# Seven products of halves in place of eight for the output projection of a hybrid encoder block

## The chip, the cores and the metric

The kernel runs on one core of a Trainium2 chip. A core has five engines with a queue each: TensorE (PE; its weight loads are listed apart as PEld), VectorE (DVE), ScalarE (ACT), GpSimd (POOL) and SyncE (SP), whose queue issues nearly all DMAs. They meet through semaphores only. The metric is the device time of one execution in microseconds (us), the median of several.

## The reference, cut to what matters

One encoder layer over 512 positions of 1024 features in float32. Two token mixers run side by side: a pooling branch and a gated delta rule. The place that is changed is where they come together:

```python
merged = jax.nn.sigmoid(g_pool) * y_pool + jax.nn.sigmoid(g_dn) * y_dn   # y_dn = o @ dn_out
x = x + merged @ w_o[l]                       # (512, 1024) @ (1024, 1024)
h2 = rmsnorm(x, norm2_w[l])
u = dwconv_centered(h2 @ ffn_up[l], ffn_conv_w[l], ffn_conv_b[l])
gate, val = jnp.split(u, 2, axis=-1)
x = x + (jax.nn.silu(gate) * val) @ ffn_down[l]
return rmsnorm(x, final_norm_w)
```

## The kernel before, in words

**Arithmetic.** Every large product is done in three matmuls. An operand is split in a high part (`hi`, a cast to fp32r by ACT) and the rest (`lo`, a subtraction by POOL or DVE); `mm3` adds hi·hi, hi·lo and lo·hi in one PSUM bank. A *triple* below is one call of `mm3`: three matmuls of 128 rows by 128 columns with 512 moving columns.

**Stages around the change.** `po_unit` forms the pooling branch's projection. `do_unit(c)` forms column block c of `o @ dn_out` (8 blocks of 8 triples, PSUM tile `ps_do`), with the tiles of `o` kept in the pool `kq` (tags `kT`, `kk`). Its weights come through `weights`: SP loads 512 KB (`wr_do`), ACT casts it (`wh_do`), POOL makes the rest in two halves (`wl_do`). Then DVE multiplies PSUM with a gate (`gdl`, L1538) and adds the pooling branch (`m1l`, L1541), ACT casts the sum (`m_hi`) and DVE forms its rest (`m_lo`, L1548). Then comes the product with `w_o`: `wo_block` loads `w_o` in eight pieces of 512 KB through the ring of raw weights, ACT casts 16 tiles and POOL makes their 16 rests (`wo_lo`, `wo_kk`, L1586). The tiles of the second half of the columns lie in `kT` and `kk`, which are free once `ps_do` is done. PE forms 4 token tiles x 2 halves of columns, each of 8 triples (`ps_wo`, 192 matmuls), and DVE adds each to x (L1624). Once both halves of a token tile are in, `norm_transpose` norms it over all 1024 features: ACT squares and sums, ACT takes the root, DVE scales (`sq`, 1024 wide, L539), PE turns it in 8 transposes (`pt_b`), and ACT and DVE split it in `h_hi`, `h_lo`. The up-projection (`ps_up`) starts on the first two token tiles, in half-width matmuls, while the last tile is being normed.

**What sets the order.** Nothing is ordered by hand. Each step is recorded as a task (`A` for ACT, `V` DVE, `G` POOL, `M` PE, `L` a DMA) with what it reads and writes, a cost and a key. `Planner.run` lays them out by a list schedule with these costs: among the tasks of an engine that are ready, the lowest key goes first (`FEED` before `EVICT` before `CHAIN` before the rest). What it finds is the fixed order of each engine's queue in the program; on the chip an engine never goes past its next instruction. Buffers of a kind form a ring, and `RINGS` says how many there are.

Of the kernel before, what the change touches and what calls it, by code (L numbers as in the profile page):

```python
# [227 lines left out]
def hybrid_block(  # L228
# [107 lines left out]
    tri = const.tile([P, 2, P], F32, name="tri")  # L336

    def causal(ap, d, pattern, fill):
        sgn = 1 if d == 0 else -1
        pool.affine_select(  # L340
            out=ap, in_=ap, compare_op=ALU.is_ge, fill=fill, base=0,
            pattern=pattern + [[sgn, P]], channel_multiplier=-sgn,
        )

    for d in range(2):
        pool.memset(tri[:, d, :], 1.0)
        causal(tri[:, d, :], d, [], 0.0)
    mask = const.tile([P, 2, P], F32, name="mask")
    for d in range(2):
        pool.memset(mask[:, d, :], 0.0)  # L350
        causal(mask[:, d, :], d, [], NEG)
# [1171 lines left out]
    def do_unit(c):
        box, pp, u = job(
            dn_out[0][:, c * P : (c + 1) * P], KD, lambda k: o_hl[k], lambda k, a, b_: [f"kT{k}", f"kk{k}"], f"do{c}"
# [14 lines left out]
        def plus():  # L1540
            dve.tensor_tensor(out=b["m1"], in0=b["gd"], in1=b["m1"], op=ALU.add)  # L1541

        def hi():
            m_hl[c] = [pools["mg"].tile([P, S], F32R, name=f"m_{n}{c}") for n in ("hi", "lo")]
            act.copy(m_hl[c][0], b["m1"])

        def lo():
            dve.tensor_tensor(out=m_hl[c][1], in0=b["m1"], in1=f32(m_hl[c][0]), op=ALU.subtract)  # L1548
# [15 lines left out]
    wo = {0: [None] * KD, 1: [None] * KD}  # L1564

    def wo_block(hf, kk, u):
        b = {}
# [15 lines left out]

        def lo(j):
            k = 2 * kk + j
            pool.tensor_tensor(out=wo[hf][k][1], in0=b["raw"][:, j, :], in1=f32(wo[hf][k][0]), op=ALU.subtract)  # L1586
# [416 lines left out]
```

## Time and profile before

| | |
|---|---|
| median of 3 runs | 882.44 us (881.97 to 883.57) |
| the profiled execution | 884.96 us, with a span of 883.2 us |
| busy share of the span | PE 99%, PEld 83%, DVE 63%, POOL 57%, ACT 52% |
| mean granted clock of PE | 0.999 |
| matmuls into `ps_do`, start | from 439.2 us to 483.2 us |
| matmuls into `ps_wo`, start | from 483.5 us to 530.0 us |
| first matmul of the up-projection | 530.2 us |

A row of the timeline gives the start in us from the span's start, the duration, the engine, the line, the operation, the tiles (out<-in), the shapes and how many instructions were merged; in brackets stands how long the engine had been idle and what ended it. Matmuls overlap, so their own duration (0.39 us) is longer than the distance from one start to the next.

### The profile page before, as it was taken

What the parts mean: (1) busy time and instruction counts of PE and PEld (TensorE: products, weight loads), DVE (VectorE), ACT (ScalarE), POOL (GpSimd) and SP (SyncE); (2) the same over time, 40 slices, a digit from 0 to 9 for tenths busy, and PEclk for the clock granted to TensorE, in tenths of its full rate; (3) what the DMA queues carried; (4) which work ended last, traced back from release to release, by engine and by line L of the source; (5) the groups of instructions that cost most, each with busy time, mean ns of one, the idle gap of its engine ahead of it and who ended that gap; (6) DMA issues with size and microseconds to landing.
All of it is one profiled execution on the core that took longest, in us unless ns stands there. A gap on an engine that the chain in (4) does not pass through costs nothing. (4 is left out here: it accounts for less than half of the span.)

```text
span 883.2 us, 13747 instructions
## 1 busy us (share of the span) xinstructions
PE 872.4 (99%) x5051; PEld 735.2 (83%) x5051; DVE 554.7 (63%) x985; ACT 457.2 (52%) x759; POOL 499.3 (57%) x438
## 2 busy tenths in 40 slices
PE   8999999999999999999999999999999999999997
PEld 7988888888888787889878888888888888888886
DVE  4657687357568797555544145655665554569996
ACT  5588554335858543345755334444443333465664
POOL 3545455324546654244467806877787764567763
PEclk9999999999999999999999999999999999999999
DMA  7265546404245453224687607666666753365554
GB/s 205 79 197 139 140 119 152 127 26 131 73 118 151 126 146 83 75 75 137 223 258 264 191 1 233 219 207 222 215 203 203 242 172 101 105 203 191 169 175 157
DMA packets 165511, 138.08 MB, mean 156 GB/s; under 512 B 23662, under 2 KB 133051, under 8 KB 165444
## 3 DMA queue, kind: packets, MB, share of 16 engines
q1 hardware_dynamic: 160706, 135.62, 49.4%
q10 hardware_dynamic: 4738, 1.58, 0.8%
q8 instruction: 40, 0.66, 0.3%
q14 instruction: 27, 0.22, 0.1%
HBM read 113.03 MB, written 24.15 MB: 155 GB/s over the span
## 5 line engine op out<-in xcount | busy, mean ns | idle before, releaser
L413 POOL TENSOR_TENSOR wl_up<-wr_up,wh_up 128x512 fp32r<-128x512 f32 x88 | 114.2, 1320 | 52.4 <-ACT wh_up L409 52.4
L389 PE MATMUL ps_up<-h_lo,wh_up 128*128 128x512 f32 (+1 forms) x368 | 139.9, 380 | 0.3 <-DVE h_lo L558 0.3
L388 PE MATMUL ps_up<-h_hi,wh_up 128*128 128x512 f32 (+1 forms) x368 | 139.9, 380 | 0.0
L390 PE MATMUL ps_up<-h_hi,wl_up 128*128 128x512 f32 (+1 forms) x368 | 139.8, 380 | 0.0
L1716 DVE SCALAR_TENSOR_TENSOR c<-ps_up,fw,c 128x511 f32<-128x511 f32 x88 | 66.0, 750 | 101.3 <-ACT c L1710 95.4
L1701 POOL TENSOR_TENSOR tp<-tp 128x512 f32<-128x512 f32 x44 | 60.4, 1373 | 39.7 <-DMA tp<-in_ffn_down_dram 34.6
L1905 POOL TENSOR_TENSOR w_dn<-wr_dn,w_dn 128x512 fp32r<-128x512 f32 x44 | 65.9, 1513 | 28.7 <-ACT w_dn L1902 27.2
L389 PEld LDWEIGHTS ps_up<-h_lo,wh_up 128*128 128x128 f32 x368 | 69.2, 188 | 13.8 <-DVE h_lo L558 0.5
L390 PEld LDWEIGHTS ps_up<-h_hi,wl_up 128*128 128x128 f32 x368 | 69.2, 188 | 13.2
L388 PEld LDWEIGHTS ps_up<-h_hi,wh_up 128*128 128x128 f32 x368 | 69.2, 188 | 13.0
L409 ACT CAST wh_up<-wr_up 128x1024 fp32r<-128x1024 f32 x44 | 46.3, 1052 | 63.3 <-issue 29.3
L1902 ACT CAST w_dn<-wr_dn 128x512 fp32r<-128x512 f32 x69 | 42.4, 621 | 29.5 <-PE dn L390 20.6
L389 PE MATMUL dn<-w_dn,as 128*128 128x512 f32 x141 | 54.2, 385 | 0.0
L388 PE MATMUL dn<-w_dn,as 128*128 128x512 f32 x141 | 54.2, 384 | 0.0
L390 PE MATMUL dn<-w_dn,as 128*128 128x512 f32 x141 | 54.2, 384 | 0.0
L1670 DVE TENSOR_TENSOR as<-a,as 128x512 fp32r<-128x512 f32 (+1 forms) x41 | 41.8, 1044 | 0.1
L413 POOL TENSOR_TENSOR wl_k<-wr_k,wh_k 128x512 fp32r<-128x512 f32 x16 | 20.2, 1286 | 33.5 <-ACT wh_k L409 33.5
L1666 ACT CAST as<-a 128x512 fp32r<-128x512 f32 (+1 forms) x41 | 21.5, 535 | 32.2 <-DVE a L1737 28.6
L413 POOL TENSOR_TENSOR wl_do<-wr_do,wh_do 128x512 fp32r<-128x512 f32 x16 | 26.0, 1647 | 15.3 <-ACT wh_do L409 15.3
L413 POOL TENSOR_TENSOR wl_gp<-wr_gp,wh_gp 128x512 fp32r<-128x512 f32 x16 | 21.9, 1389 | 22.1 <-ACT wh_gp L409 22.1
L413 POOL TENSOR_TENSOR wl_v<-wr_v,wh_v 128x512 fp32r<-128x512 f32 x16 | 21.3, 1353 | 22.6 <-ACT wh_v L409 22.6
L1710 ACT ACTIVATE c<-ps_up,fw 128x512 f32<-128x512 f32 x44 | 33.9, 770 | 0.0
(358 smaller groups left out, 2421.0 us busy)
## 6 DMA issues: line engine op xcount, KB each, us to landing
wr_up<-in_ffn_up_dram SPq DMA_DIRECT2D x44, 512.0 KB, 3.8
tp<-in_ffn_down_dram SPq DMA_DIRECT2D x22, 512.0 KB, 5.8
t_scr<-tp SPq DMA_DIRECT2D x44, 256.0 KB, 2.8
wr_dn<-t_scr SPq DMA_DIRECT2D x20, 512.0 KB, 3.8
wr_dn<-in_ffn_down_dram SPq DMA_DIRECT2D x15, 512.0 KB, 3.6
x<-in_x_dram SPq DMA_DIRECT2D x8, 512.0 KB, 5.4
wr_k<-in_w_in_dram SPq DMA_DIRECT2D x8, 512.0 KB, 4.7
wr_z<-in_w_in_dram SPq DMA_DIRECT2D x8, 512.0 KB, 3.7
```

What stands on the lines that cost most here:

```text
L388: pe.matmul(ps, ahi, bhi, start=first, stop=False)
L389: pe.matmul(ps, ahi, blo, start=False, stop=False)
L390: pe.matmul(ps, alo, bhi, start=False, stop=last)
L409: act.copy(b["hi"], b["raw"])
L413: pool.tensor_tensor(out=b["lo"][:, sl], in0=b["raw"][:, sl], in1=f32(b["hi"][:, sl]), op=ALU.subtract)
L1666: act.copy(sets[p][:, i : i + n, 0, :], src())
L1670: dve.tensor_tensor(out=w[:, :, 1, :], in0=src(), in1=f32(w[:, :, 0, :]), op=ALU.subtract)
L1701: G(cp(512), lambda o=o, x=x, y=y: pool.tensor_tensor(out=w(*o), in0=w(*x), in1=w(*y), op=ALU.subtract), r=[n(*x), n(*y)], w=[n(*o)], key=u)
L1710: act.activation(b[j], box["ps"], AF.Identity, scale=fw[:, 1, ci : ci + 1], bias=fw[:, 3, ci : ci + 1])
L1716: dve.scalar_tensor_tensor(out=y[:, lo:hi], in0=box["ps"][:, lo + sh : hi + sh], scalar=fw[:, k, ci : ci + 1], in1=y[:, lo:hi], op0=ALU.mu ...
L1902: act.copy(b["w"][:, 0, :], raw["t"][:, j, :])
L1905: eng.tensor_tensor(out=b["w"][:, 1, :], in0=raw["t"][:, j, :], in1=f32(b["w"][:, 0, :]), op=ALU.subtract)
```

## The change

`merged` (512 x 1024) and `w_o` (1024 x 1024) are cut in four blocks each. Seven products of combinations of blocks take the place of the eight products of blocks. A product is 2 token tiles x 4 triples of 512 columns. The order of the products is 1, 2, 6, 5, 3, 7, 4 (`W_ORDER`).

- The raw `w_o` no longer passes through the ring; it is loaded into the memory of `h` (`wr_hi`, `wr_lo`), which is free after the last projection of `h`, and its eight loads are paced by `po_unit` and the first two `do_unit`s.
- Combinations of its blocks: 16 subtractions of 512 columns (`wsum`, L1588), 8 of them on DVE and 8 on POOL. 28 casts by ACT (16 before) and 28 rests (`wsplit`, L1604), 23 on POOL and 5 on DVE.
- `merged` stays as one f32 tile `m` (`plus`, L1549). Combinations of its blocks are 8 instructions of DVE (`mcombine`, L1620, two row blocks of 256 tokens at a time), and the operands are split in 15 casts of ACT and 15 rests of DVE (`msplit`, L1632, tile `ms`), where before there were 8 and 8.
- PSUM: products 1, 6, 3 and 4 use two banks of `oo` (tile `wo`), 2, 5 and 7 the ring `pp`. Sums go to x by 12 additions of DVE from PSUM (`wplus`, L1753; 8 before), or first into a tile `wu` (one cast of ACT and two additions of DVE for each token half, L1765), and from there to x by 6 additions of POOL.
- The second norm is taken in two halves of its features: `norm2_first` squares the half that is ready first and lets POOL multiply it with the weight (L1697), `norm2_rest` squares the other half, takes the root, scales the first half on ACT and the other on DVE (L1712, 512 wide). The transposes are as many as before.
- In `do_unit` the sigmoid, the multiplication and the addition have other keys, the POOL half of `wl_do` is planned 0.2 us longer (`more`), the weights of the first up-projection block have another key, and the masks `tri`, `mask` lie in another pool.

**POOL, from the weights of dn_out's third column block on.** Before:

```order
L413 TENSOR_TENSOR wl_do_4590<-wr_do_4437,wh_do_4589 128x512 x2
L413 TENSOR_TENSOR wl_do_4617<-wr_do_4499,wh_do_4616 128x512 x2
L413 TENSOR_TENSOR wl_do_4665<-wr_do_4554,wh_do_4664 128x512 x2
L413 TENSOR_TENSOR wl_do_4709<-wr_do_4625,wh_do_4708 128x512 x2
L413 TENSOR_TENSOR wl_do_4753<-wr_do_4655,wh_do_4752 128x512 x2
L1586 TENSOR_TENSOR wo_lo_4793<-wo_r_4743,wo_hi_4792 128x512
L413 TENSOR_TENSOR wl_do_4801<-wr_do_4699,wh_do_4800 128x512 x2
```

and now, from two rests of `w_o` ahead of the same place:

```order
L1604 TENSOR_TENSOR ws_lo_4587<-wr_hi,ws_hi_4586 128x512
L415 TENSOR_TENSOR wl_do_4599<-wr_do_4444,wh_do_4598 128x512 x2
L415 TENSOR_TENSOR wl_do_4631<-wr_do_4498,wh_do_4630 128x512 x2
L1604 TENSOR_TENSOR ws_lo_4612<-wr_hi,ws_hi_4611 128x512
L1604 TENSOR_TENSOR ws_lo_4620<-wr_hi,ws_hi_4619 128x512
L1604 TENSOR_TENSOR ws_lo_4676<-wr_hi,ws_hi_4675 128x512
L415 TENSOR_TENSOR wl_do_4685<-wr_do_4547,wh_do_4684 128x512 x2
L1604 TENSOR_TENSOR ws_lo_4696<-wr_hi,ws_hi_4695 128x512
L415 TENSOR_TENSOR wl_do_4735<-wr_do_4643,wh_do_4734 128x512 x2
L1604 TENSOR_TENSOR ws_lo_4761<-wr_hi,ws_hi_4760 128x512
L415 TENSOR_TENSOR wl_do_4781<-wr_do_4668,wh_do_4780 128x512 x2
```

Work on `w_o` now stands between the weights of dn_out's blocks. From `wl_do` of the second block to `wl_up` of the second up-projection block, ends included, POOL has 60 instructions of 512 columns (35 before): 14 `wl_do`, one `o_lo`, 23 rests and 8 combinations of `w_o`, 6 additions to x, 4 multiplications of the norm, 4 `wl_up`.

**DVE, from the eviction of dn_out's last column block on.** Before:

```order
L1538 TENSOR_TENSOR gdl_4782<-ps_do_4845,gdl_4782 128x512
L1541 TENSOR_TENSOR m1l_4815<-gdl_4782,m1l_4815 128x512
L1548 TENSOR_TENSOR m_lo_4915<-m1l_4815,m_hi_4914 128x512
L1624 TENSOR_TENSOR x_0_4573<-ps_wo_4892,x_0_4573 128x512
L1624 TENSOR_TENSOR x_1_4574<-ps_wo_4934,x_1_4574 128x512
```

and now:

```order
L1546 TENSOR_TENSOR gdl_4828<-ps_do_4867,gdl_4828 128x512
L1753 TENSOR_TENSOR x_1_4571<-wo,x_1_4571 128x512
L1604 TENSOR_TENSOR ws_lo_4969<-wr_lo,ws_hi_4968 128x512
L1549 TENSOR_TENSOR m<-gdl_4828,m1l_4882 128x512
L1632 TENSOR_TENSOR ms_4979<-m,ms_4979 128x2x256
L1620 TENSOR_TENSOR m<-m 128x2x256
L1632 TENSOR_TENSOR ms_4887<-m,ms_4887 128x256
L1620 TENSOR_TENSOR m<-m 128x2x256 x2
L1753 TENSOR_TENSOR x_0_4570<-ps_wo_4971,x_0_4570 128x512
L1632 TENSOR_TENSOR ms_4979<-m,ms_4979 128x2x256
```

Before, three instructions (two of them with both inputs in SBUF) lay between the last `ps_do` and the last operand of the product with `w_o`. Now the second half of product 6's left operand (`ms_4979`) stands behind eleven, eight of them with both inputs in SBUF.

**PE, where product 6 starts** (`wo<-wq_...,ms_4979`) and product 2 ends (`ps_wo_4971`, `ps_wo_4995<-...,ms_4887`). Now, with none like it before:

```order
L391 MATMUL ps_wo_4995<-ws_hi_4760,ms_4887 128x512
L389 MATMUL wo<-wq_kT_4878,ms_4979 128x512
L390 MATMUL wo<-wq_kk_4879,ms_4979 128x512
L391 MATMUL wo<-wq_kT_4878,ms_4979 128x512
L389 MATMUL wo<-wq_kT_4898,ms_4979 128x512
L390 MATMUL wo<-wq_kk_4899,ms_4979 128x512
L389 MATMUL ps_wo_4971<-ws_hi_4767,ms_4887 128x512
L389 MATMUL ps_wo_4995<-ws_hi_4767,ms_4887 128x512
L389 MATMUL wo<-wq_kT_4898,ms_4979 128x512
```

(rows that repeat are left out). From the end of `ps_do` to the first triple that needs the second half of `ms_4979`, PE has 57 matmuls. The whole program has 24 rows fewer on PE, 3729 for 3753.

The diff, cut to its core:

```diff
-    def weights(src, kt, n, name, u):
+    def weights(src, kt, n, name, u, feed=None, more=0.0):
+        feed = FEED + u if feed is None else feed
...
     def do_unit(c):
         box, pp, u = job(
-            dn_out[0][:, c * P : (c + 1) * P], KD, lambda k: o_hl[k], lambda k, a, b_: [f"kT{k}", f"kk{k}"], f"do{c}"
+            dn_out[0][:, c * P : (c + 1) * P], KD, lambda k: o_hl[k], lambda k, a, b_: [f"kT{k}", f"kk{k}"], f"do{c}", more=0.2
         )
...
-        V(cd(512), mul, r=[pp], w=[f"y:lgd{c}"], key=EVICT + u)
-        V(cd(512), plus, r=[f"y:lgd{c}"], w=[f"y:lm1{c}"], key=EVICT + u)
-        A(ca(512), hi, r=[f"y:lm1{c}", "pool:xp"], w=[f"mhi{c}"], key=EVICT + u)
-        V(cd(512), lo, r=[f"y:lm1{c}", f"mhi{c}"], w=[f"mlo{c}"], key=EVICT + u)
+        V(cd(512), mul, r=[pp], w=[f"y:lgd{c}"], key=FEED + u)
+        V(cd(512), plus, r=[f"y:lgd{c}", f"y:lm1{c}", "pool:xp"], w=[f"m{c}#0", f"m{c}#1"], key=FEED + u)
...
+    W_ORDER = (1, 2, 6, 5, 3, 7, 4)
+    W_HOME = {1: "a", 2: "b", 6: "q0", 5: "q4", 3: "a", 7: "b", 4: "q0"}
...
+    def wsum(dst, x, y, key, eng=G):
+        e, cost = (pool, cp(512) + 0.15) if eng is G else (dve, cd(512) + 0.3)
+        eng(cost, lambda: e.tensor_tensor(out=dst[0](), in0=x[0](), in1=y[0](), op=ALU.subtract),
+            r=[x[1], y[1], *(["pool:xp"] if dst[1][0] == "t" else [])], w=[dst[1]], key=key)
+
+    def wsplit(p, k, src, key, eng=G):
...
+        A(ca(512), hi, r=[src[1], "pool:xp"], w=names, key=key)
+        eng(cost, lo, r=[src[1], names[0]], w=[names[1]], key=key)
...
+    def msplit(p, i, n, src, srcn, key):
...
+        A(ca(256 * n), hi, r=srcn, w=names, key=key)
+        V(cd(256 * n) + 0.25, lo, r=srcn, w=names, key=key)
...
+    LO_BY = {1: (G, G, G, G), 2: (G, G, G, G), 6: (G, V, G, G), 5: (G, G, G, G), 3: (G, V, G, G), 7: (G, V, G, G), 4: (G, V, G, V)}
+    wsplits(1)
+    for k in range(QK):
+        wsum(quad(1, k), quad(1, k), quad(0, k), WORK + u_wo[2] - 30 + k, V)
+        wsum(t24(k), quad(1, k + QK), quad(1, k), WORK + u_wo[2] - 20 + k, V)
+        wsum(quad(0, k), t24(k), quad(0, k), WORK + u_wo[5] + 10 + k)
...
+    for i in range(0, QK, 2):
+        (x, xn), (y, yn), (z, zn) = mblk(i, 0, 2), mblk(i, 1, 2), mblk(i + QK, 1, 2)
+        mcombine(y, yn, y, z, yn + zn, ALU.add, FEED + u_wo[6] + i, 2)
+        mcombine(x, xn, y, x, xn + yn, ALU.subtract, FEED + u_wo[6] + i, 2)
+        msplit(6, i, 2, x, xn, FEED + u_wo[6] + i)
...
+    def norm2_rest(t, u):
...
+        A(ca(512), lambda: act.activation(b["sq"][0], b["sq"][0], AF.Copy, scale=b["rst"]), r=[f"n2{t}"], w=[sqn(t, 0)], key=u - 40)
+        V(cd(512) + 0.3, scale, r=[f"n2{t}", f"xr{t}#{hl}", "n2b"], w=[sqn(t, 1)], key=u - 40)
...
+    for p in W_ORDER:
+        u = u_wo[p]
         for j in range(2):
+            for k in range(QK):
+                M(MM3, lambda p=p, k=k, j=j: wmm(p, k, j), r=[f"ms:{p}#{k}", *wnames(p, k)], w=[wname(p, j)], key=u + 10 * j + k)
+            wdone(p, j, ADD + u + 10 * j)
```

More of the change, by code (lines that the diff above doesn't have):

```diff
@@ L335, in hybrid_block @@
     ones_r = const.tile([P, P], F32R, name="ones_r")
[L336 to L351, printed above, removed]
     edges = const.tile([P, 4, 16], F32, name="edges")
@@ L375, in hybrid_block, with causal @@
     open_pool("st")
+    tri = pools["qv"].tile([P, 2, P], F32, name="tri")
+    def causal(ap, d, pattern, fill):
+        sgn = 1 if d == 0 else -1
+        pool.affine_select(
+            out=ap, in_=ap, compare_op=ALU.is_ge, fill=fill, base=0,
+            pattern=pattern + [[sgn, P]], channel_multiplier=-sgn,
+        )
+    for d in range(2):
+        pool.memset(tri[:, d, :], 1.0)
+        causal(tri[:, d, :], d, [], 0.0)
+    mask = pools["qv"].tile([P, 2, P], F32, name="mask")
+    for d in range(2):
+        pool.memset(mask[:, d, :], 0.0)
+        causal(mask[:, d, :], d, [], NEG)
     def ring(pool_name, tag, shape, dt, name):
@@ L447, in job @@
         else:
-            wb, whi, wlo = weights(src, kt, n, name, u)
+            wb, whi, wlo = weights(src, kt, n, name, u, feed, more)
         pp = f"pp:{name}"
@@ L1510, in hybrid_block @@
     x2 = [None] * NT
-    m_hl = [None] * KD
+    QK = KD // 2
+    wr, mg = [None, None], {}
+    Z(lambda: wr.__setitem__(slice(None), [hp.tile([P, KD, S], F32, tag=f"h_{n}", name=f"wr_{n}") for n in ("hi", "lo")]),
+      w=["wr"], after=["h"])
     def merge_open():
@@ new lines, in hybrid_block, with wo_load @@
+    W_ORDER = (1, 2, 6, 5, 3, 7, 4)
+    W_HOME = {1: "a", 2: "b", 6: "q0", 5: "q4", 3: "a", 7: "b", 4: "q0"}
+    WORK = CHAIN + 3000
+    ADD = EVICT - 60
+    T_W = (slice(0, 256), slice(256, 512))
+    u_wo = {p: next_unit() for p in W_ORDER}
+    u_w0 = u_wo[1]
+    wsets, wslot = {}, {}
+    def wo_load(n, kk):
+        sp.dma_start(
+            wr[n][:, 2 * kk : 2 * kk + 2, :],
+            w_o[0][kk * 256 : (kk + 1) * 256, n * 512 : (n + 1) * 512].rearrange("(k p) c -> p k c", p=P),
+        )
@@ new lines, in wsplit, with hi, lo @@
+    def wsplit(p, k, src, key, eng=G):
+        home = W_HOME[p]
+        def hi():
+            if home[0] == "q":
+                i = int(home[1:]) + k
+                w = [kq.tile([P, S], F32R, tag=f"{n}{i}", name=f"wq_{n}{p}{k}") for n in ("kT", "kk")]
+            else:
+                w = [pools["mg"].tile([P, S], F32R, tag=f"ws_{n}{home}{k}", name=f"ws_{n}{p}{k}") for n in ("hi", "lo")]
+            wslot[p, k] = w
+            act.copy(w[0], src[0]())
+        def lo():
+            e.tensor_tensor(out=wslot[p, k][1], in0=src[0](), in1=f32(wslot[p, k][0]), op=ALU.subtract)
+        e, cost = (pool, cp(512) + 0.15) if eng is G else (dve, cd(512) + 0.3)
+        names = wnames(p, k)
+        A(ca(512), hi, r=[src[1], "pool:xp"], w=names, key=key)
+        eng(cost, lo, r=[src[1], names[0]], w=[names[1]], key=key)
@@ new lines, in hybrid_block @@
+    for i in range(0, QK, 2):
+        (x, xn), (z, zn) = mblk(i, 0, 2), mblk(i + QK, 0, 2)
+        mcombine(x, xn, z, x, xn + zn, ALU.subtract, FEED + u_wo[3] + i, 2)
+        msplit(3, i, 2, x, xn, FEED + u_wo[3] + i)
+    for p, src in ((7, s3), (4, lambda i: mblk(i + QK, 1, 2))):
+        for i in range(0, QK, 2):
+            msplit(p, i, 2, *src(i), FEED + u_wo[p] + i)
+    h2 = []
+    n2 = {}
+    early = lambda t: 1 if t > 1 else 0
+    half = lambda hf: slice(hf * 512, (hf + 1) * 512)
@@ new lines, in hybrid_block, with wname, wmm @@
+    wacc = {}
+    def wname(p, j):
+        return f"oo:wo#{j}" if p in (1, 6, 3, 4) else f"pp:wo{p}{j}"
+    def wmm(p, k, j):
+        name = wname(p, j)
+        if p == 1 and "oo" not in wacc:
+            wacc["oo"] = banks2("wo")
+        if name[0] == "p" and k == 0:
+            wacc[name] = bank("pp", f"ps_wo{p}{j}")
+        wacc[p, j] = wacc["oo"][:, j, :] if name[0] == "o" else wacc[name]
+        a, ts_ = wsets[p], slice(j * P, (j + 1) * P)
+        mm3(wacc[p, j], a[:, k, 0, ts_], a[:, k, 1, ts_], *wslot[p, k], k == 0, k == QK - 1)
```

204 lines of the change are left out of this document (129 added, 75 removed).

## The prediction

> **What bounds the kernel now.** I read the engines' busy time and the chain of waits first, then the windows around the change, then the timelines of PE, POOL and DVE in them.
>
> ```profile
> span 883.2 us, 13747 instructions
> PE 872.4 (99%) x5051; PEld 735.2 (83%) x5051; DVE 554.7 (63%) x985; ACT 457.2 (52%) x759; POOL 499.3 (57%) x438
> PE 48%; DVE 0%; ACT 0%; DVEq 0%; issue 0%
> ...
> core 0: us, PE busy (x) PEld busy (x) DVE busy (x) ACT busy (x) POOL busy (x), PEclk, DMA share, GB/s
> 384.00:434.00 50.00, 50.00 (x297) 43.81 (x297) 28.60 (x50) 30.58 (x46) 22.26 (x17) 1.00 0.42 139
> 434.00:484.00 50.00, 49.83 (x219) 40.52 (x218) 21.64 (x27) 27.07 (x38) 34.82 (x23) 1.00 0.82 267
> 484.00:531.00 47.00, 47.00 (x222) 38.83 (x221) 15.68 (x23) 16.87 (x29) 20.20 (x16) 1.00 0.30 95
> ```
>
> PE is busy 99% of the span and no other engine holds a whole per cent of the chain. In the two windows of the change, the product with dn_out and the product with w_o, PE is busy 96.83 of 97 us at a granted clock of 1.00. So matmuls that are taken away shorten the kernel, as long as PE's operands still come in time; everything that the change adds lands on POOL (42 idle us in the 97), DVE (60) and ACT (53). Whether that idle time can be used is the question.
>
> **What is removed.** Where one half of the columns ends and the other begins, and where the first transposes stand, PE shows:
>
> ```profile
> 483.22 0.40 PE L390 MATMUL ps_do<-o_hi,wl_do 128*128 128x512 f32 x1
> 483.45 0.39 PE L388 MATMUL ps_wo<-wo_hi,m_hi 128*128 128x512 f32 x1
> ...
> 499.78 0.40 PE L388 MATMUL ps_wo<-wo_kT,m_hi 128*128 128x512 f32 x1
> ...
> 530.23 0.28 PE L388 MATMUL ps_up<-h_hi,wh_up 128*128 128x256 f32 x1
> ```
>
> The 72 matmuls from 483.45 to 499.78 stand 0.227 us apart; the 120 from there to 530.23 take 30.45 us with three token tiles' transposes among them (1.04 each, by a row below), so 0.228 each. The 24 that go are worth 24 x 0.227 to 0.228 = **-5.5 us**. That is all there is to win: 0.6%.
>
> **What is added to POOL and DVE.** The order gives POOL 60 instructions of 512 columns for 35 in the stretch that ends with the weights of the second up-projection block. DVE gets, in the same stretch, 48 instructions of 512 columns whose inputs both lie in SBUF (8 additions to m, 8 combinations of w_o, 8 of m, 15 rests of m, 5 rests of w_o, 4 scalings). What one costs depends on the other engine:
>
> ```profile
> 489.14 10.05 POOL L1586 TENSOR_TENSOR wo_kk<-wo_r,wo_kT 128x512 fp32r<-128x512 f32 x8
> 449.17 6.78 POOL L413 TENSOR_TENSOR wl_do<-wr_do,wh_do 128x512 fp32r<-128x512 f32 x4 [1.72 <-ACT wh_do L409]
> ...
> 449.00 0.69 DVE L1541 TENSOR_TENSOR m1l<-gdl,m1l 128x512 f32<-128x512 f32 x1
> 450.44 0.96 DVE L1548 TENSOR_TENSOR m_lo<-m1l,m_hi 128x512 fp32r<-128x512 f32 x1 [0.74 <-ACT m_hi L1545]
> 451.31 0.68 DVE L1538 TENSOR_TENSOR gdl<-ps_do,gdl 128x512 f32<-128x512 f32 x1
> 452.03 1.07 DVE L1541 TENSOR_TENSOR m1l<-gdl,m1l 128x512 f32<-128x512 f32 x1
> 453.78 1.01 DVE L1548 TENSOR_TENSOR m_lo<-m1l,m_hi 128x512 fp32r<-128x512 f32 x1 [0.69 <-ACT m_hi L1545]
> ...
> 795.95 3.53 POOL L1905 TENSOR_TENSOR w_dn<-wr_dn,w_dn 128x512 fp32r<-128x512 f32 x2 [1.07 <-ACT w_dn L1902]
> 795.35 2.98 DVE L1670 TENSOR_TENSOR as<-a,as 128x512 fp32r<-128x512 f32 x3
> ...
> L1538 DVE TENSOR_TENSOR gdl<-ps_do,gdl x8: 679/692/692, 448.3 to 483.7; 128x512 f32<-128x512 f32 x8
> L1541 DVE TENSOR_TENSOR m1l<-gdl,m1l x8: 692/694/1293, 449.0 to 484.4; 128x512 f32<-128x512 f32 x8
> ```
>
> Eight POOL instructions alone take 10.05 us, 1.256 each. From 449.17 to 455.95 four take 6.78, 1.70 each; in that stretch lie four two-input instructions of DVE, so each of these took (6.78 - 4 x 1.256) / 4 = 0.44 from POOL. At 795.95 two POOL instructions beside three of DVE take 1.77 each. DVE pays too: 0.69 alone, 0.96 to 1.29 beside POOL. The eviction `gdl`, which reads PSUM and SBUF, costs 0.68 to 0.69 in all eight cases: what is shared is the reading of SBUF by two-input DVE work and by POOL. I take 0.45 per DVE instruction; the ends are 0 (every one falls in a POOL gap) and 0.69 (it keeps POOL out for all of its time).
>
> The Trainium skill, "SBUF — State Buffer", section "Who interferes with whom", has this as a rule: a DVE instruction with two SBUF inputs and a GpSimd instruction that reads SBUF exclude each other by a lock, and the later one blocks fully. The pairs above agree in kind, but show less than a full block, 0.44 for 0.69.
>
> The stretch on POOL then lasts 60 x 1.256 + 48 x 0.45 = 75.4 + 21.6 = 97.0 us if POOL is never without work. Its start and the place where PE needs its last result:
>
> ```profile
> 437.18 1.29 POOL L1294 TENSOR_TENSOR o_lo<-ob,o_hi 128x512 fp32r<-128x512 f32 x1
> 443.20 2.99 POOL L413 TENSOR_TENSOR wl_do<-wr_do,wh_do 128x512 fp32r<-128x512 f32 x2 [4.72 <-ACT wh_do L409]
> ...
> 534.13 5.38 POOL L1701 TENSOR_TENSOR tp<-tp 128x512 f32<-128x512 f32 x4 [29.93 <-DMA tp<-in_ffn_down_dram]
> ...
> 533.10 0.28 PE L388 MATMUL ps_up<-h_hi,wh_up 128*128 128x256 f32 x1
> ...
> 535.62 1.04 PE L550 MATMUL pt_b<-ident,sq 128*128 128x128 f32 x8
> ```
>
> It starts between 438.5 (437.18 + 1.29) and 443.2 (where the second block's cast was waited for), so it ends between 535.5 and 540.2. The last instruction of it is the second half of the second block's `wl_up`; PE needs that at that block's fifth k. Before, PE stood there at 533.10 + 12 x 0.12 = 534.5, or 535.6 with the eight transposes (1.04) that now stand ahead of it. With 24 matmuls fewer it would be there at 530.1. POOL thus comes 5.4 to 10.1 us late: the time against before is **-0.1 to +4.6 us** at this place, and POOL's 29.93 us of rest before 534.13 are used up. I take an end at 538.5, since the stretch's first weights still wait for their cast: **+2.9 us**. By POOL alone (75.4) it would end at 513.9 to 518.6 and bind nothing.
>
> **Where PE waits on the way.** These stalls are part of the same 8.4 us (5.5 + 2.9), not added to them.
>
> *Product 6.* Its left operand's second half stands eleven instructions behind the last eviction of `ps_do` on DVE: eight two-input, three one-input.
>
> ```profile
> 483.65 0.69 DVE L1538 TENSOR_TENSOR gdl<-ps_do,gdl 128x512 f32<-128x512 f32 x1 [1.72 <-PE ps_do L390]
> 478.93 1.29 DVE L1541 TENSOR_TENSOR m1l<-gdl,m1l 128x512 f32<-128x512 f32 x1
> ...
> L1548 DVE TENSOR_TENSOR m_lo<-m1l,m_hi x8: 956/1015/1021, 450.4 to 485.8; 128x512 fp32r<-128x512 f32 x8
> L413 POOL TENSOR_TENSOR wl_do<-wr_do,wh_do x16: 1286/1737/1756, 434.4 to 475.4; 128x512 fp32r<-128x512 f32 x16
> ```
>
> DVE starts there 0.2 after PE has gone on (483.65, 483.45). PE has 57 matmuls before it needs the operand: 57 x 0.227 = 12.9 us. With POOL busy without a gap, DVE gets one instruction in per POOL instruction, so 8 x 1.70 + 3 x 0.69 + 0.2 = 15.9, less some 0.3 for one of half the width: 15.6, a stall of 2.7. If the eight cost 0.69 it is 7.8 and nothing waits. It decides at a mean of (12.9 - 2.3) / 8 = 1.33 us; `m_lo`, with POOL busy 34.82 of 50 us, had about 1.01. What is queued behind it on DVE: the evictions of product 2, then product 5's operands. *Norm.* From product 3's first half to the transposes of `sq_01` PE has 48 matmuls and four transposes, 11.4 us; DVE six two-input and three one-input instructions and a reciprocal, 12.4 beside POOL, 6.4 without: a stall of 0 to 1.0, 1.0 taken.
>
> *dn_out.* Rests of w_o now stand between the `wl_do`, up to three in a row.
>
> ```profile
> 462.83 3.33 POOL L413 TENSOR_TENSOR wl_do<-wr_do,wh_do 128x512 fp32r<-128x512 f32 x2 [2.11 <-ACT wh_do L409]
> ...
> L1902 ACT CAST w_dn<-wr_dn 128x512 fp32r<-128x512 f32 x69 | 42.4, 621 | 29.5 <-PE dn L390 20.6
> ```
>
> POOL used to wait 2.1 us in a block; one rest fits in there, three (5.1) make a block 3.0 late if PE has no lead. I take a stall of 0.5, ends 0 and 3.0, nearer to 0 since there is about one rest a block on the mean. So 4.2 of the 8.4 us are met before the up-projection, and 4.2 there, behind `wl_up`. *At no cost:* ACT's 19 casts more (0.62 for one of 512 columns, 12 us) lie in 53 idle us; without that cover they would be on the path with the operands they make. The eight loads of w_o, 4.2 MB, move from behind the loads of dn_out, past them on SP's queue, to the window from 384 on, whose DMA share is 0.42; the one they leave had 0.82. The halved norm's scaling (2 x 0.69 for 1.28) is equal work.
>
> **Sum.** The profiled execution took 884.96 us (span 883.2, 1.8 around it). 884.96 - 5.5 + 8.4 = 887.9. The median of the runs, 882.44, is 2.5 lower, so **885.3**.
>
> **Rivals.** *A, the forecast: the shared reads make POOL the bound, 885.3* (883 to 888 for ends of 535.5 + 0.7 and 541). For it: no POOL gap is left in the sum. Against: 97.0 rests on all 48 meeting POOL.
>
> *B, faster: the DVE work falls into POOL's gaps.* One place: DVE's queue ahead of product 6, and from there the rests. POOL waits for casts in the dn_out stage (4.72, 1.72 above), and DVE's instructions that land there cost POOL nothing. If the eight have a mean under 1.33 us and POOL's end comes before 530.1 (a stretch of at most 530.1 - 441.5 = 88.6, that is (88.6 - 75.4) / 48 = 0.27 for each DVE instruction), only the 0.5 of dn_out is left: 884.96 - 5.5 + 0.5 - 2.5 = **877.4**.
>
> *C, a draw:* 0.38 for each (a stretch of 93.6 from 441.5 ends at 535.1, 5.0 late): 884.96 - 5.5 + 5.0 - 2.5 = **882**.
>
> *D, heavier:* POOL stands still for 0.55 of each DVE instruction: 75.4 + 26.4 = 101.8, an end at 543.3, 4.8 later than A: **890**; for all of its 0.69, 108.5, an end at 550 and 897. The 0.44 measured speaks against the upper end. The rule of the Trainium skill's page "SBUF — State Buffer" named above, taken in full, is that upper end.
>
> That the matmuls aren't removed is excluded by the order, with 24 rows fewer.
>
> **How the numbers follow.** A 0.56, B 0.22, C 0.12, D 0.10. A measurement of this kernel can tell 0.2% (1.8 us) from no change, so "same" is 880.7 to 884.2. A gives 0.44 slower and 0.12 same (its lower end); B 0.22 faster; C 0.10 same, 0.02 faster; D 0.10 slower: faster 0.24, same 0.22, slower 0.54. The range leaves out half of B's lower spread and the upper half of D: 877 to 890; A's own is 883 to 888.
>
> **What would show it.** Right: 5027 matmul records or near; POOL busy from about 440 to 538 with hardly a gap and `ws_lo` and `wq_kk` at a mean near 1.6 us; two-input DVE rows at 1.2 us or more; PE idle behind `ms_4979` (2 to 3 us), at the transposes (about 1) and behind `wl_up` at the second up-projection block. Wrong: POOL done before 530, PE without idle time between 484 and 531, DVE rows near 0.7 (then B); or PE waiting mainly inside dn_out for `wl_do`, or for a load, which I have at 0.5 and 0.

## The result and the profile after

The changed kernel takes 887.11 us (median of 6; 885.91 to 889.61), the kernel before in the same comparison 882.66: a ratio of 1.0054, with a 95% interval of 1.0037 to 1.0072. It is slower by some 4.5 us, where 2.9 were forecast, and the time lies in the range.

The page, and the windows of the two stretches of the change (columns as in the prediction), of the kernel after:

```profile
span 884.5 us, 13820 instructions
PE 867.1 (98%) x5027; PEld 729.3 (82%) x5027; DVE 602.2 (68%) x1025; ACT 471.1 (53%) x792; POOL 542.2 (61%) x463
...
434.00:484.00 50.00, 49.71 (x218) 40.59 (x217) 35.73 (x32) 28.17 (x42) 47.02 (x32) 1.00 0.92 298
484.00:531.00 47.00, 39.97 (x171) 29.97 (x170) 42.07 (x48) 25.68 (x52) 44.03 (x29) 1.00 0.04 12
```

The 24 matmuls are gone (5027 for 5051). POOL is busy 91.05 of 97 us where it was 55.02, DVE 77.80 where it was 37.32, and PE, which had no idle time to speak of, lacks 7.03 us in the second window.

The spans of the two profiled executions (884.5 and 883.2) differ by 1.3 us only. They must not be compared as they stand, since the execution before began late: PE has 83 matmuls in its first 20 us, and 102 in the execution after. The first and last stage that hold the change between them, of before and of after (duration of one, first and last start):

```profile
L388 PE MATMUL ps_do<-o_hi,wh_do x64: 388/389/397, 439.2 to 482.8; 128*128 128x512 f32 x64
L388 PE MATMUL dn<-w_dn,as x141: 278/389/396, 771.9 to 865.5; 128*128 128x512 f32 x135, 128*128 128x256 f32 x6
```

```profile
L389 PE MATMUL ps_do<-o_hi,wh_do x64: 388/389/397, 436.6 to 480.8; 128*128 128x512 f32 x64
L389 PE MATMUL dn<-w_dn,as x141: 277/389/396, 772.8 to 866.4; 128*128 128x512 f32 x135, 128*128 128x256 f32 x6
```

From the start of dn_out's product to the start of the down-projection it is 332.7 before and 336.2 after, 3.5 us more. That is the change. The 2.6 us ahead of it belong to the execution and not to the change (e4 below has the changed code there, and its profiled execution has only 85 matmuls in its first 20 us). The profiled execution after took 886.23 us, 0.9 less than the median, which is most of what lies between 3.5 here and 4.5 by the medians. In what follows the distance from dn_out to the down-projection is called the *stretch*.

What PE waited for in it, of the kernel after (total idle time, times, longest):

```profile
PE wo L389 <- DVE x L1753: 3.0, 3, 1.5
PE wo L391 <- DVE ms L1632: 1.8, 2, 1.3
PE ps_wo L391 <- DVE ms L1632: 0.7, 1, 0.7
PE wo L389 <- ACT wu L1760: 0.7, 1, 0.7
PE wo L389 <- ACT ms L1628: 0.4, 1, 0.4
PE ps_do L391 <- POOL wl_do L415: 0.3, 1, 0.3
```

These nine waits are 6.9 us of idle time. A wait costs some 0.27 more than its row shows, because a matmul's own 0.39 hides the start of it and the next one starts 0.34 instead of 0.23 later: 492.64 to 494.37 and 494.71 below are 2.07 for 0.46, a loss of 1.6 for an idle time of 1.34. Measured by such distances the nine cost 9.3 us. The transposes lose 0.7 (two groups of four start 0.87 and 0.83 apart, at 0.13 for one), and the kernel before had lost 1.3 in waits: 9.3 + 0.7 - 1.3 - 5.5 = 3.2 of the 3.5 us. Below, a single wait is given by its first distance alone, 0.11 less than by this reckoning.

Two kinds of wait can be seen. One was forecast: product 6 and product 2 wait for `ms`, 3.6 us by distances (1.50 for the first half of product 6's operand, 0.92 in product 2, 0.62 and 0.58 for the second half of product 6's operand). PE, and DVE ahead of it:

```profile
492.64 0.39 PE L390 MATMUL wo<-wq_kk,ms 128*128 128x512 f32 x1
494.37 0.51 PE L391 MATMUL wo<-wq_kT,ms 128*128 128x512 f32 x1 [1.34 <-DVE ms L1632]
494.71 0.39 PE L389 MATMUL wo<-wq_kT,ms 128*128 128x512 f32 x1
...
488.58 0.69 DVE L1753 TENSOR_TENSOR x<-wo,x 128x512 f32<-128x512 f32 x1 [2.51 <-ACT ws_hi L1601]
489.19 1.73 DVE L1604 TENSOR_TENSOR ws_lo<-wr_lo,ws_hi 128x512 fp32r<-128x512 f32 x1
490.85 1.78 DVE L1549 TENSOR_TENSOR m<-gdl,m1l 128x512 f32<-128x512 f32 x1
492.55 1.76 DVE L1632 TENSOR_TENSOR ms<-m,ms 128x512 fp32r<-128x512 f32 x1
```

Each of these two-input instructions of DVE takes 1.7 to 1.8, as summed; the one that reads PSUM takes 0.69.

The other kind was not in the prediction: PE waits for `x`, an *eviction*, in the middle of a product:

```profile
484.03 0.39 PE L391 MATMUL wo<-ws_hi,ms 128*128 128x512 f32 x1
485.20 0.50 PE L389 MATMUL wo<-ws_hi,ms 128*128 128x512 f32 x1 [0.78 <-DVE x L1753]
486.83 0.50 PE L389 MATMUL wo<-ws_hi,ms 128*128 128x512 f32 x1 [0.68 <-ACT wu L1760]
...
484.45 0.69 DVE L1753 TENSOR_TENSOR x<-wo,x 128x512 f32<-128x512 f32 x1 [0.46 <-PE wo L391]
486.20 0.59 ACT L1760 COPY wu<-wo 128x512 f32<-128x512 f32 x1 [1.23 <-PE wo L391]
```

PE is at the second triple of product 1's second token tile, and DVE reads the finished first one. They work on different banks, but both banks are one tile, `wo`. The waits follow the tile and not the bank: the matmul waits for the read to end (485.14), ACT's copy then waits for that triple to end, and the next matmul waits for ACT. Run e1 tests this. The planner counts the two banks as two things and knows of no such wait. It comes at products 1, 3 and 4: 0.94, 0.85, 0.94 and 1.50 by distances, 4.2 us.

POOL's stretch was the bound of the forecast. Its first and last instruction, and the two waits in it:

```profile
437.72 3.00 POOL L415 TENSOR_TENSOR wl_do<-wr_do,wh_do 128x512 fp32r<-128x512 f32 x2 [2.25 <-ACT wh_do L411]
443.16 3.01 POOL L1604 TENSOR_TENSOR ws_lo<-wr_hi,ws_hi 128x512 fp32r<-128x512 f32 x2 [0.73 <-ACT ws_hi L1601]
501.41 1.87 POOL L1604 TENSOR_TENSOR ws_lo<-wr_hi,ws_hi 128x512 fp32r<-128x512 f32 x1 [2.85 <-ACT ws_hi L1601]
532.46 1.74 POOL L415 TENSOR_TENSOR wl_up<-wr_up,wh_up 128x512 fp32r<-128x512 f32 x1
```

It runs from 437.72 to 534.20, 96.5 us, 3.6 of them idle. PE did not wait for its end, since PE was late itself.

### The profile page after: what moved, and what is told of

It reads as the page before. It is cut to its first block, busy times and chain, and to the rows that moved or that the text cites. A ratio compares the mean times of both kernels' runs of the same rounds, so it can differ in the third digit from the quotient of the medians.

```text
span 884.5 us, 13820 instructions
## 1 busy us (share of the span) xinstructions
PE 867.1 (98%) x5027; PEld 729.3 (82%) x5027; DVE 602.2 (68%) x1025; ACT 471.1 (53%) x792; POOL 542.2 (61%) x463
## 4 chain that ended last, share of the span: by engine, by line
PE 62%; DVE 3%; ACT 1%; issue 0%; POOL 0%; DVEq 0%
PE ps_up L389 9%; PE ps_up L390 9%; PE ps_up L391 9%; PE dn L389 4%; PE dn L391 4%; PE dn L390 4%; PE ps_do L391 2%; PE ps_do L389 2%; PE ps_do L390 2%; PE ps_gp L389 1%; PE ps_gp L391 1%; PE ps_gp L390 1%; PE ps_p L389 1%; PE ps_po L391 1%; PE ps_po L389 1%; PE ps_po L390 1%
## 5 line engine op out<-in xcount | busy, mean ns | idle before, releaser
L415 POOL TENSOR_TENSOR wl_up<-wr_up,wh_up 128x512 fp32r<-128x512 f32 x88 | 117.0, 1350 | 46.4 <-ACT wh_up L411 46.3
L1831 DVE TENSOR_TENSOR as<-a,as 128x512 fp32r<-128x512 f32 (+1 forms) x41 | 38.5, 964 | 0.1
L1900 ACT ACTIVATE c<-c 128x512 f32<-128x512 f32 x22 | 13.9, 633 | 35.4 <-DVE c L1877 35.3
```

What stands on the lines that cost most here:

```text
L415: pool.tensor_tensor(out=b["lo"][:, sl], in0=b["raw"][:, sl], in1=f32(b["hi"][:, sl]), op=ALU.subtract)
L1831: dve.tensor_tensor(out=w[:, :, 1, :], in0=src(), in1=f32(w[:, :, 0, :]), op=ALU.subtract)
```

## The experiments

Two theories stood against each other: **R**, the shared reading of SBUF by DVE and POOL sets the pace; **T**, the waits at the common PSUM tile do. All times are medians; the ratio is to the kernel before on the same chip (882.4 to 882.9 there).

| run | edit to which kernel | us | ratio, 95% interval |
|---|---|---|---|
| e1 | changed: two one-bank tiles | 885.86 | 1.0032 (1.0022 to 1.0043) |
| e2 | changed: 23 DVE reads from PSUM, work left out | 880.57 | 0.9969 (0.9959 to 0.9979) |
| e3 | e1 and e2 | 877.62 | 0.9937 (0.9920 to 0.9954) |
| e4 | e1, sum of dn_out from PSUM | 884.87 | 1.0029 (1.0018 to 1.0040) |
| e6 | e4, operands of 5, 6, 3 in PSUM | 881.66 | 0.9982 (0.9971 to 0.9993) |
| e7 | e6, other planner costs | 878.13 | 0.9943 (0.9928 to 0.9958) |
| e8 | e6, a second set of costs | 877.51 | 0.9935 (0.9919 to 0.9951) |
| e9 | changed: norm at once | 889.37 | 1.0071 (1.0055 to 1.0088) |
| e10 | e8: 15 DVE reads back to SBUF, work left out | 884.69 | 1.0025 (1.0015 to 1.0035) |
| e11 | e8: one two-bank tile again | 883.36 | 1.0002 (0.9991 to 1.0013) |
| e12 | changed, one execution more | 888.23 | |
| e13 | changed: the costs and the choice of rests of e8 alone | 889.59 | 1.0086 (1.0069 to 1.0103) |

### Two one-bank tiles (e1)

```diff
-            wacc["oo"] = banks2("wo")
+            close_pool("po2")
+            open_pool("po1", space=bass.MemoryType.PSUM)
+            wacc["oo"] = [pools["po1"].tile([P, 512], F32, tag=f"oo{i}", name=f"wo{i}") for i in range(2)]
...
-        wacc[p, j] = wacc["oo"][:, j, :] if name[0] == "o" else wacc[name]
+        wacc[p, j] = wacc["oo"][j] if name[0] == "o" else wacc[name]
```

> The changed kernel with one edit: the two PSUM banks in which products 1, 6, 3 and 4 are summed are two tiles of one bank each, where the changed kernel has one tile of two banks. Order and arithmetic are the same. In the trace of the change PE's second token tile of products 1, 3 and 4 starts or goes on only after DVE (and ACT for product 1) has read the first token tile's bank: distances of 1.17, 1.07, 1.17 and 1.73 us between matmuls that else stand 0.23 apart, 4.2 us in all. Theory T (the common tile makes these waits, and they cost what they last): they vanish, 887.1 - 4.2 = 882.9; DVE, which stood idle for 2.5 us behind the first of them (488.58), is earlier too, so the 3.6 us of waits for product 6's and 2's operands (ms) shrink by up to 2.5: down to 880.4. Theory R (reading SBUF by DVE and POOL in turn sets the pace, as predicted; the waits at the common tile only stand where PE would have waited anyway): 886 to 888, and PE waits longer behind ms and behind wl_up.

885.86: a little below R's range (886 to 888) and 3 us above the most that T allows (882.9). It is 1.2 us below the changed kernel, and the two intervals overlap. The waits at `x` are all gone, with the order of every engine as it was, so their cause is shown. But PE now comes to product 6 two microseconds sooner and waits there; DVE, without a pause from 487.04 on, is the limit. PE's waits in the stretch, and then PE around the longest of them and a window behind it:

```profile
PE wo L393 <- DVE ms L1634: 2.8, 2, 2.0
PE ps_wo L393 <- DVE ms L1634: 0.8, 1, 0.8
...
497.55 0.40 PE L392 MATMUL wo<-wq_kk,ms 128*128 128x512 f32 x1
499.93 0.79 PE L393 MATMUL wo<-wq_kT,ms 128*128 128x512 f32 x1 [1.98 <-DVE ms L1634]
500.52 0.63 PE L391 MATMUL wo<-wq_kT,ms 128*128 128x512 f32 x1
500.94 0.63 PE L392 MATMUL wo<-wq_kk,ms 128*128 128x512 f32 x1
...
500.00:506.00 6.00, 6.00 (x14) 4.71 (x15) 5.79 (x6) 1.40 (x3) 3.57 (x3) 0.50 0.00 0
```

A third thing shows: behind the wait of 1.98 us the matmuls stand 0.43 apart for 6 us, and the granted clock is 0.50 there. Fifteen matmuls at 0.2 more each cost 3.0 us, so in this execution what the edit gave was partly taken back by the clock: the stretch is 336.4 us (336.2 in the kernel after), and would be 333.4 without it.

### Reads from PSUM in place of SBUF (e2, e3)

```diff
-        V(cd(256 * n) + 0.22, lambda: dve.tensor_tensor(out=dst(), in0=x(), in1=y(), op=op), r=names, w=dstn, key=key)
+        def combine():
+            z = from_psum()[:, 0 : 256 * n].rearrange("p (k t) -> p k t", t=256)
+            dve.tensor_tensor(out=dst(), in0=z, in1=y(), op=op)
+
+        V(cd(256 * n) + 0.22, combine, r=names, w=dstn, key=key)
...
-            dve.tensor_tensor(out=w[:, :, 1, :], in0=src(), in1=f32(w[:, :, 0, :]), op=ALU.subtract)
+            dve.tensor_tensor(out=w[:, :, 1, :], in0=z, in1=f32(w[:, :, 0, :]), op=ALU.subtract)
```

> The changed kernel with one edit: the 8 combinations and the 15 rests of m on DVE take one of their two inputs from a PSUM bank that holds zeros, so 23 of the 48 DVE instructions no longer read two SBUF operands. Left out: the arithmetic of these 23, so the output is not the layer's; order and counts are the same but for one memset. Theory R (shared reads): these rows take 0.69 us where they took 1.2 to 1.8; POOL's stretch gets shorter by up to 23 x 0.45 = 10 us; PE's 3.6 us of waits for ms and most of the 0.7 at the transposes go, the waits at the common PSUM tile (4.2) stay: 887.1 - 4 = 883. Theory T alone (the reads don't matter): 887, the waits for ms stay. If both waits have one cause, the lateness of DVE, the waits at the common tile go as well: 879 to 881.

> Both edits together: two one-bank tiles, and 23 DVE instructions with one input from PSUM (arithmetic of the combinations and rests of m left out). Theory R and T as two causes that add up: 887.1 - 4.2 - 4 = 879, some 3.5 us below the kernel before (882.7), and PE in the stretch has waits of under 1.5 us. If there is a third cause (weights of dn_out, loads), the time stays above 881 and the waits show it. The 24 matmuls alone would give 882.7 - 5.5 = 877.2.

880.57 and 877.62: 6.5 and 9.5 us below the changed kernel. The rests of m from 484 to 531, grouped, of the kernel after and of e2:

```profile
L1632 DVE TENSOR_TENSOR ms<-m,ms 128x512 fp32r<-128x512 f32 (+1 forms) x10 | 11.4, 1172 | 0.0
L1620 DVE TENSOR_TENSOR m<-m 128x512 f32<-128x512 f32 x4 | 5.9, 1499 | 0.0
```

```profile
L1645 DVE TENSOR_TENSOR ms<-zero,ms 128x512 fp32r<-128x512 f32 (+1 forms) x12 | 7.3, 636 | 0.1
L1630 DVE TENSOR_TENSOR m<-zero,m 128x512 f32<-128x512 f32 x4 | 2.6, 674 | 0.0
```

The same instructions in the same order take half as long once one input lies in PSUM, and PE no longer waits for `ms` at all. The gain is larger than R forecast for this run (6.5 for 4). The time lies where the third case of the expectation, one cause for both kinds of wait, put it (879 to 881), but what that case says of the waits does not hold: those at the common tile shrink (`x` from 3.0 to 1.6) and do not go. What waits are left in e2 are those at the common tile and one for a rest of w_o:

```profile
PE wo L389 <- DVE x L1766: 1.6, 2, 0.8
PE ps_wo L390 <- DVE ws_lo L1604: 1.5, 1, 1.5
PE wo L389 <- ACT wu L1773: 0.7, 1, 0.7
```

With the tiles split as well (e3) the view lists no wait in the stretch, and the time is 5.3 us below the kernel before, which is what 24 matmuls are worth. So there is no third cause of size.

### The sum of dn_out from PSUM (e4)

```diff
-            dve.tensor_tensor(out=b["gd"], in0=box["ps"], in1=b["gd"], op=ALU.mult)
+            dve.tensor_tensor(out=box["ps"], in0=box["ps"], in1=b["gd"], op=ALU.mult)
...
-            dve.tensor_tensor(out=mg["m"][:, c, :], in0=b["gd"], in1=b["m1"], op=ALU.add)
+            dve.tensor_tensor(out=mg["m"][:, c, :], in0=box["ps"], in1=b["m1"], op=ALU.add)
```

> Two one-bank tiles, and the gated product of dn_out is written back to its PSUM bank, so that the 8 additions m = gdl + m1l have one SBUF input; full arithmetic. The planner lays the stretch out anew for it (the norm's small tiles get four buffers, which the new order needs). Theory R: 8 of 48 DVE instructions no longer keep POOL out (8 x 0.45 = 3.6 us of POOL's stretch), DVE itself gains up to 8 x 1.0 us around the evictions: 1 to 2 us below the kernel with two tiles alone. Theory T: the same time as that kernel within 1 us, since PE does not wait there.

884.87, 1.0 below e1; the intervals overlap, so this run decides nothing between R and T.

### A kernel that keeps the arithmetic (e6, e7, e8)

```diff
-        mcombine(y, yn, y, z, yn + zn, ALU.add, FEED + u_wo[6] + i, 2)
-        mcombine(x, xn, y, x, xn + yn, ALU.subtract, FEED + u_wo[6] + i, 2)
-        msplit(6, i, 2, x, xn, FEED + u_wo[6] + i)
+        (a, an), (b_, bn) = in_bank(f"cy{i}"), in_bank(f"cx{i}") if i < 2 else (x, xn)
+        mcombine(a, an, y, z, yn + zn, ALU.add, FEED + u_wo[6] + i, 2)
+        mcombine(b_, bn, a, x, xn + an, ALU.subtract, FEED + u_wo[6] + i, 2)
+        msplit(6, i, 2, b_, bn, FEED + u_wo[6] + i)
```

(`in_bank` gives a bank of the ring `ds`, which stands empty until the transposes; products 5 and 3 read there too.) In e7 and e8 the planner's costs differ: POOL's work on w_o +0.05 for +0.15, its part of the norm +0.4 or +0.3 for 0, DVE's combinations +0.1 for +0.22, and in e8 also DVE's rests of w_o +0.4 for +0.3, its scaling +0.1 for +0.3, and no `more`.

> Full arithmetic. Two one-bank tiles for the sums; the gated product of dn_out goes back to its PSUM bank (as in the run e4); and product 5's operand (both blocks) and products 6's and 3's operand (the first of two blocks) are formed in PSUM banks that stand empty until the transposes, so their casts read PSUM and 7 of the 15 combinations and rests around product 6 have one SBUF input. 15 of the 48 DVE instructions no longer shut POOL out. Theory: reading SBUF in turn is the main cause (23 such instructions gave -6.5 us and, with two tiles, -9.5). 15 of 23, but those nearest to PE's waits: 3 to 5 us below the changed kernel with two tiles (885.9): 881 to 883. Rival: the waits move to POOL's rests of w_o and to the norm, whose reads are untouched: 884 to 885, as e4.

> As the run before it, with four other costs in the planner (POOL's combinations and rests of w_o 0.1 us cheaper, the norm's weighting on POOL 0.4 dearer, DVE's combinations 0.12 cheaper, so that the order of the queues changes); same instructions. If what is left of the waits comes from the order in which DVE and POOL take turns, 1 to 3 us below the run before it, 879 to 882, and faster than the kernel before (882.9). If the sum of the shared reads sets it, the same as the run before it within 1 us.

> As e7 with costs chosen a second way, and the rests of w_o that DVE makes are two of product 6 (one before) and none of product 3 (one before). Same expectation as for e7: 879 to 882 if the order of turns matters, else as e6.

881.66 as expected, 878.13 and 877.51. The last is faster than both kernels: 9.6 us below the changed one, 5.4 below the one before. The last two took less than the expectation's lower end (879). In the stretch of e8 PE has one wait, and POOL is busy 89.58 of 97 us:

```profile
PE pt_b L1735 <- ACT sq L1729: 0.8, 1, 0.8
...
434.00:484.00 50.00, 50.00 (x222) 41.34 (x221) 32.87 (x37) 30.28 (x46) 46.96 (x33) 1.00 0.90 296
484.00:531.00 47.00, 46.19 (x248) 38.96 (x247) 37.62 (x54) 27.52 (x58) 42.62 (x29) 1.00 0.10 28
```

POOL has its 60 instructions as before, but is through with them in 89.2 us (437.45 to 526.63) where the kernel after took 96.5. So their number does not make the loss; what each of them and of DVE's loses to the other does.

### Each edit taken back from e8 (e10, e11)

e10 reads a small SBUF tile in the 15 places where e8 reads PSUM (`in0=ident...` for `in0=box["ps"]`, and likewise in `mcombine` and `msplit`); e11 is the diff of e1 backwards.

> The fastest kernel so far (e8, 877.5) in the same order on every engine, with one edit: the 15 DVE instructions that had been given one input in PSUM (8 additions to m, 3 combinations, 4 rests) read a small SBUF tile in its place. Left out: their arithmetic. Theory of the shared reads: POOL loses 15 x 0.45 = 6.8 us, DVE some 0.5 us or more in each; e8's gain of 5.4 over the kernel before is used up: 881 to 886, and PE waits behind ms and behind POOL's rests again. Rival (the new order alone made e8 fast): 877 to 879.

> e8 with the one tile of two PSUM banks back in place of the two tiles of one bank; full arithmetic, same order. The wait at the common tile as measured between the two kernels with reads left out (880.6 and 877.6): 2 to 4 us, so 879.5 to 881.5. If those waits hide each other here: 877 to 878.5.

884.69 and 883.36: 7.2 and 5.9 us lost. The order on the engines is the same in all three, so the order alone did not make e8 fast. In e10 POOL's 60 instructions take 95.8 us (438.14 to 533.90), 6.6 more than in e8: 0.44 for each of the 15 reads, the price of the prediction. That e10 repeats a small tile shows no cost of its own: its 15 instructions take 1.17 to 1.79, where two-input ones of the changed kernel beside POOL take up to 1.78. e11 lost more than the 2 to 4 expected; why was not tested (e8's order may let PE run closer to the evictions). PE's waits of e10, and then of e11:

```profile
PE ps_wo L393 <- DVE ms L1640: 2.1, 1, 2.1
PE pt_b L1741 <- ACT sq L1735: 1.2, 1, 1.2
PE ps_do L393 <- POOL wl_do L417: 0.6, 3, 0.3
```

```profile
PE wo L389 <- DVE x L1764: 2.4, 3, 0.9
PE wo L389 <- DVE wu L1776: 0.8, 1, 0.8
PE wo L389 <- ACT wu L1771: 0.7, 1, 0.7
```

### The order alone, and the norm alone (e13, e9)

> The changed kernel with the planner's costs and the two-for-one choice of rests of e8, but with its reads and its two-bank tile as they were (the norm's small tiles get four buffers). Full arithmetic. Theory: what made e8 fast are the 15 DVE instructions with one SBUF input and the two tiles; the order alone leaves 60 instructions on POOL and 48 two-input ones on DVE: 885 to 890. Rival: the order alone is worth the 4.1 us that lie between the kernels e6 and e8: 882 to 884.

889.59: e8's costs and choice of rests on the changed kernel's reads and tile are 2.5 us worse than the changed kernel. (The planner makes an order of them that differs in places from e8's; the same order is what e10 and e11 have.) The 4.1 us between e6 and e8 are not to be had while the reads and the tile are as they were.

e9 squares both halves of a token tile when both are there and scales both on DVE:

```diff
-        G(cp(512), weigh, r=[f"xr{t}#{hf}", "n2b"], w=[sqn(t, 0)], key=u)
...
+        for i, hf in ((0, 1 - hl), (1, hl)):
+            V(cd(512) + 0.3, lambda i=i, hf=hf: scale(i, hf), r=[f"n2{t}", f"xr{t}#{hf}", "n2b"], w=[sqn(t, i)], key=u - 40)
```

> The changed kernel with its second norm taken at once, as before the change: both halves are squared only when both are there, and DVE scales both (POOL's 4 multiplications and ACT's 4 scalings are gone, DVE has 4 more two-input instructions; the two-bank tile stays). If the seven products with their operands make the loss: within 1 us of the changed kernel (887.1), 0.6 later for a second square, up to 5 us less work on POOL. If the halved norm makes it: under 885.

889.37, 2.3 us above the changed kernel, where within 1 us was expected; the intervals overlap, so whether the halved norm gains time is not shown. The 885 that would have made it the cause of the loss is excluded: it is no part of the loss.

### The changed kernel once more (e12)

> The changed kernel once more, unaltered. Its executions lay between 885.9 and 889.6, with a mean granted clock of 0.997 in the two quickest and 0.992 to 0.995 in the others; its profile (0.997) has no stretch at half clock. In the kernel with two tiles and in the one with the reads put back, a wait of 2.0 and 2.1 us is followed by 3 to 6 us in which the matmuls stand 0.43 us apart for 0.23. Theory: the slower executions of the changed kernel have such a stretch, 10 to 25 matmuls x 0.2 = 2 to 5 us. If this execution is one of the slower, its profile shows granted clock 0.5 somewhere between 490 and 506; if it is one of the quick ones (886), nothing is told.

888.23 us at a mean clock of 0.994. Its profile has the waits of the one above, and one thing more, behind the last wait at the common tile:

```profile
527.99 0.80 PE L389 MATMUL wo<-wq_kT,ms 128*128 128x512 f32 x1 [1.46 <-DVE x L1753]
528.58 0.63 PE L390 MATMUL wo<-wq_kk,ms 128*128 128x512 f32 x1
...
527.00:532.00 5.00, 4.01 (x13) 3.24 (x14) 2.73 (x6) 2.06 (x5) 4.52 (x4) 0.66 0.00 0
```

From 527.99 to 531.3 PE runs at half clock, where the first profile, with the same wait (1.46, at 527.68), does not. It stands at 527 to 532, later than the expectation had it, and costs about 1.4 us (six matmuls and four transposes). This holds for two executions that were profiled. That the others differ for the same reason is not shown, and their mean clocks do not tell: one of 886.74 us has 0.994 too, and e4's profile has 0.994 without any half clock in the stretch (0.83 in its first 20 us, for 0.91 in the first profile of the changed kernel).

## Why the prediction was right, and where it was not

**Matmuls saved: right.** 5.5 us; e3 and e8, without waits, are 5.3 and 5.4 below the kernel before.

**Shared reads: right in kind, and nearly in price.** Two-input DVE instructions took 1.50 to 1.78 from 489 to 496 where 1.70 was used. POOL's stretch took 96.5 us for 97.0, but this match is partly luck: 92.9 of them are busy, (92.9 - 75.4) / 48 = 0.36 for each DVE instruction in place of 0.45, since some fell in a pause of POOL, and 3.6 idle us, which the sum did not have, made up for it. Where reads were put back (e10) the price is 0.44. Taking 23 reads away gives 6.5 us, putting 15 back costs 7.2. The Trainium skill, "SBUF — State Buffer", section "Who interferes with whom", calls what the two share an exclusive lock: whichever issues first has it for the whole instruction, and the other blocks. DVE's rows agree: 1.78 is a POOL instruction of 1.26 and some 0.5 of its own. For POOL, rows at a mean of 1.65 (`ws_lo`) show a loss of 0.4 each, not the 0.69 of a DVE instruction's whole length.

**Product 6: right in kind, short in size, and partly by luck.** One stall of 2.7 was forecast, at the second half of `ms_4979`. PE lost 3.6 behind `ms` by then: 1.50 at the first half, 0.92 in product 2, 1.20 at the second half. DVE's eleven instructions took 15.5 us (485.39 to 500.93) for the sum's 15.4, but not as summed: seven two-input ones took 1.49 each and the eighth 0.68, not 1.70, and DVE stood idle for 2.51 ahead of 488.58. The row there names ACT, but what it reads, product 1's second token tile, was only then finished (488.10 + 0.39), late by the waits at the common tile.

**The norm and dn_out: right.** 1.0 forecast for the transposes and 0.7 measured; 0.5 for dn_out and 0.45 measured (the wait of 0.3 for `wl_do`).

**The end of POOL's stretch: wrong.** "4.2 there, behind `wl_up`" was half of the 8.4 us. PE waited for `wl_up` not at all: its last half was there at 534.20, and PE used it two microseconds later. In the place of these 4.2 stand 4.2 of another cause, the tile of two banks, of which the prediction says nothing though the change names it ("two banks of `oo`, tile `wo`"). A bound from an engine's amount of work is a lower bound on the end; it does not say that PE will meet it. The sum came out near by this coincidence, and the forecast of the sign rests on it in part: e1, without the tile's waits, is still slower than before, but in its profile only by little when the half clock is left out (333.4 us for the stretch against 332.7).

**The clock: missing.** The prediction takes 1.00 throughout. Stretches at half clock cost 3.0 us in the profile of e1 and 1.4 in that of e12. Part of the 1.8 us between the forecast 885.3 and the measured 887.1 may be of this kind; the first profile of the changed kernel, at 886.23, has none.

**Rival B** (all work hidden, 877.4) is the time that e8 reaches, 877.5, by another way: its DVE work does not fall into POOL's gaps, but reads PSUM. The condition that B set, a mean of DVE's two-input instructions ahead of product 6 under 1.33, the changed kernel misses at 1.49 (seven from 489.19 to 499.65), and PE waits there.

## What to carry to other kernels

Before work is moved to two idle engines, see whether they slow each other: here a two-input DVE instruction on SBUF that met POOL cost POOL some 0.4 us and itself up to 1.1. Giving DVE one input in PSUM (a bank that is empty anyway, the eviction written back in place) brought it back to 0.7. Two accumulators that are filled and drained in turn should be two tiles: in one tile of two banks PE waited for readers of the other bank, and a planner that counts banks did not see it. When a saving on PE gives nothing, look at the first wait on PE and at the one that takes its place when it is removed: two tiles alone gave 1.2 us here, and 3.0 once the reads were out of the way (e2 to e3).
